# A decoder layer on one core: branch for crowded experts at the fifth pair, embedding blocks spaced, eleven tiles loaded at routing, products of ones between two-row products

## The chip, the cores and the metric

The kernel runs on one core of one Trainium2 chip, in one launch. The core has five engines with a queue each: TensorE (PE; its weight loads are shown as PEld), VectorE (DVE), ScalarE (ACT), GpSimd (POOL) and SyncE (SP), which here issues all DMAs. The metric is the time of one execution on the device in microseconds (us), as the median of several runs.

## The reference, cut to what matters

All of it is fp32, for 256 tokens of width 2048 and one layer.

```python
h = x @ w_in[i]                               # 2048 -> 9216, split into u, v, q, k, vb, ga, gb
# branch A: gated causal mixing over 128 positions; branch B: stick-breaking attention
mix = (sigmoid(ga) * ya + sigmoid(gb) * yb) @ w_o[i]
x = _layer_norm(ALPHA * x + mix, ln1_g[i], ln1_b[i])
expert_idx, gate_w = _route(xf, router_w, router_bias)    # 2 of 16 experts for each token
ffn = _moe(...)                               # (silu(x @ w_gate[e]) * (x @ w_up[e])) @ w_down[e]
ple = sigmoid(x @ ple_w_gate[i]) * (p[i] @ ple_w_proj[i]) # embedding of the layer
x = _layer_norm(ALPHA * x + ffn + ple, ln2_g[i], ln2_b[i])
```

An expert's three matrices are 2048 x 1024, 2048 x 1024 and 1024 x 2048. All sixteen experts are read, 403 MB of weights; an expert may get any number of tokens.

## The kernel before, in words

**Stages.** Up to about 600 us the kernel works on the token mixing: each weight piece is split by ScalarE and VectorE into a high and a low part, and TensorE multiplies with both. Then come the first norm and the routing (lines 510 to 663), and from about 626 us the experts. They are taken as eight pairs, numbered g = 0 to 7 (`for g in range(NP)`, line 980). Each expert has 64 places (CAP); the two experts of a pair use the two halves of TensorE's columns at the same time. A pair has four phases: `inner` "A" and "B" (line 806), eight weight tiles each, make the hidden units; `outer` "0" and "1" (line 817), four tiles each, make the output columns 0 to 1023 and 1024 to 2047. `hidden` and `turn_hidden` (lines 828, 838) stand between them. `evac` (line 847) copies an outer half out of PSUM as a high part `yh` (ScalarE) and a low part `yl` (VectorE) for each of two column blocks, and four `scatter`s (line 861) add it to `acc`: a product with the selection matrix on TensorE and an add on VectorE. The scatters of outer half "0" run as events in steps 1 to 4 of outer half "1"; those of "1" are kept in `back` and run in the next pair's phase A.

**Embedding blocks.** `ple(i)` (line 760) computes 256 of the 2048 columns of the embedding term from one weight tile and a quarter megabyte of `ple_w_proj` (in `wpt`). The list `PLE` (line 31) says after which phase of which pair each of the eight blocks runs; at (6, "B") the last one stands before outer half "0" of pair 6.

**Tiles and loads.** The pool `big` has 12 buffers of 128 x 4096 fp32 (2 MB). Weight tiles come through it in a fixed order (`loads`), one 2 MB DMA each. `done` (line 152) gives a tile's buffer back and `prefetch` (line 142) issues the next loads while `live + reserve` is below 12; `keep` reserves a buffer for something else, and `BR` takes it. A load waits on SyncE until the last reader of its buffer has finished. At routing the buffers hold `x1` (the normed rows) and `xg` (the gathered tokens of two pairs), so ten weight tiles are loaded ahead. Later `acc`, the two parts of `x1`, and `x1T` take buffers, and seven are left for weights. The pool `tp` (line 41) has five buffers of 128 x 512 fp32 for `s`, `r`, `yh`, `yl` and other short-lived tiles (`S`, line 55).

**Order of the work.** The schedule is written by hand: every engine runs its instructions in the order of the program, and the framework puts the semaphore waits in. Small jobs (gathering the next pair's tokens, the residual) stand in a list `bg`, of which `step` (line 800) takes one after each half tile.

**The branch.** `overflow` (line 927) reads the largest number of tokens of an expert into a register of each engine. If it is above 64, a loop works off the rest of all pairs with weights that it loads anew. With these inputs the branch is not taken. It stands before pair 7, in line 1007, and two buffers (`ow`, `og`) are reserved for it.

**The end.** The second norm's gain and bias, two rows of 2048 numbers, are loaded into a large tile `rows` during pair 6 and spread over the partitions by GpSimd into `gb2` (lines 1010 to 1032). After the last scatter, `busy(16)` runs sixteen products of ones that nothing reads. Then the mean and the bias come in as products with two rows (line 1072), and the eight output blocks are stored.

Of the kernel before, what the change touches and what calls it, by code (L numbers as in the profile page):

```python
# [27 lines left out]
NP = NE // 2  # L28
NB = 12

PLE = [(2, "A"), (2, "1"), (3, "A"), (4, "A"), (4, "1"), (5, "A"), (6, "A"), (6, "B")]


@with_exitstack
def trunk(ctx, tc, I, out):
# [28 lines left out]
    def C(name, shape, dt=F32):  # L64
        return consts.tile(shape, dt, name=name)
# [56 lines left out]
        keep(-1)  # L122
        return B(name, dt)

    wpt = C("wpt", [128, 2, 2, 256])

    def load_one():
        key, parts = loads[state["next"]]
        t = B("w")
        for sl, src in parts:  # L130
            if state["next"] == len(loads) - 1:
                for h in (slice(0, 2048), slice(2048, 4096)):
                    SP.dma_start(t[:, h], src[:, h])
            else:
                SP.dma_start(t[:, sl], src)  # L135
        if key[0] == "ple":
            SP.dma_start(wpt[:, key[1] % 2], I["ple_w_proj"][key[1]])
        tiles[key] = t
        state["next"] += 1
        state["out"] = state.get("out", 0) + 1  # L140
# [57 lines left out]
    POOL.iota(jp, pattern=[[1, 128]], base=0, channel_multiplier=-1, allow_small_or_imprecise_dtypes=True)  # L198
    ident = C("ident", [128, 128])
    DVE.tensor_scalar(ident, jp, 0.0, None, op0=OP.is_equal)  # L200
    tail = C("tail", [128, 128])
    DVE.tensor_scalar(tail, jp, 0.0, None, op0=OP.is_le)
    capm = C("capm", [128, 128])
    DVE.tensor_scalar(capm, jp, 0.0, None, op0=OP.is_gt)
    before = C("before", [128, 128], BF)
    DVE.tensor_copy(before, capm)
    DVE.tensor_scalar(capm, capm, 4.0e30, -1.0e30, op0=OP.mult, op1=OP.add)
    ones = C("ones", [128, 128])
    DVE.memset(ones, 1.0)
    ones_b = C("ones_b", [128, 128], BF)  # L210
    DVE.memset(ones_b, 1.0)
# [304 lines left out]
        if i == 2:  # L516
            DVE.tensor_tensor(rwg, rw, gc[:, 0, :, None].to_broadcast([128, DC, 32]), op=OP.mult)
    free(3)
    xgs = B("xg").rearrange("p (h c s) -> p h c s", h=2, c=DC)
    prefetch()  # L520

    for a in range(2):
# [140 lines left out]
        DVE.tensor_copy(cmi, cmax)  # L663


    long = {}
    Pm = C("Pm", [128, 2, 2, 128], F32R)
    PO = C("PO", [128, 2, T], F32R)
    wc = C("wc", [128, NP + 1])
    hTs = [C(f"hT{k}", [128, 4, 128]) for k in range(2)]  # L670
    pT = C("pT", [128, 2, T])
    SP.dma_start(pT, I["pT"])

    def onehot(P, at):
        for a in range(2):
# [84 lines left out]
    def ple(i):  # L760
        x1T = long["x1T"]
        w = take(("ple", i)).rearrange("p (c f) -> p c f", c=DC)
        cs = slice(i * 256, (i + 1) * 256)
        pw = AUX()
        for a in range(2):
            for c in range(2):
                PE.matmul(pw[:, a * 256:(a + 1) * 256], pT[:, c, a * 128:(a + 1) * 128], wpt[:, i % 2, c, :],
                          start=(c == 0), stop=(c == 1))
        ps = MM()
        for c in range(DC):  # L770
            for a in range(2):
                PE.matmul(ps[:, a * 256:(a + 1) * 256], x1T[:, c, a * 128:(a + 1) * 128], w[:, c, :],  # L772
                          start=(c == 0 and a == 0), stop=(c == DC - 1), skip_group_check=True)
            if c % 8 == 7:
                pop_bg()
        s = S("s")
        ACT.activation(s, ps, AF.Sigmoid)
        DVE.tensor_mul(s, s, pw)
        POOL.tensor_add(long["acc"][:, :, cs], long["acc"][:, :, cs], s.rearrange("p (a f) -> p a f", a=2))
        if i == len(PLE) - 1:  # L780
            free()
            keep()
        done()


# [102 lines left out]
    frs = C("frs", [128, 2, 2])  # L888
    cw = C("cw", [128, 2, 2])
    DVE.memset(cw, 1.0)  # L890
    rowc = C("rowc", [2, T])

    def last_columns(g, at):
        pend = None
# [32 lines left out]
    def overflow():  # L927
        most = nc.values_load(cmi[0:1, 0:1], min_val=0, max_val=T)
        with tc.If(most > CAP):
            with tc.For_i(0, NP, 1) as g:  # L930
                ce = C("ce", [128, 2, 2, 2])
                one = bass.ds(g, 1)
                for k, src in enumerate((pos, wA)):
                    DVE.tensor_copy(ce[:, k, :, None, :], src.rearrange("p a (g e) -> p a g e", e=2)[:, :, one, :])
                ow = B("ow").rearrange("p (k f) -> p k f", k=2)
                xg = B("og")[:, 0:2048].rearrange("p (c s) -> p c s", c=DC)
                with tc.For_i(1, T // CAP, 1):
                    DVE.tensor_scalar(ce[:, 0], ce[:, 0], -float(CAP), None, op0=OP.add)
                    P = Pm[:, 0]
                    onehot(P, ce[:, 0])  # L940
                    selection(P, ce[:, 1], 0, NP)
                    for f in gathers(P, xg):
                        f()
                    n = 0

                    def row(i, c):
                        nonlocal n
                        n += 1
                        SP.dma_start(ow[:, n % 2, :], xw[one, i + c // 2].rearrange("o p f -> p (o f)")[
                            :, (c % 2) * 2048:(c % 2 + 1) * 2048])  # L950
                        return ow[:, n % 2, :]

                    for k in range(2):
                        ps = [MM(), MM()]
                        for c in range(DC):
                            mm_gu(ps, xg[:, c, :], row(8 * k, c).rearrange("p (e k f) -> p e k f", e=2, k=2), c)
                        turn_hidden(hidden(ps, NP), hTs[k])
                    for k in range(2):
                        ps = [MM(), MM()]
                        for fc in range(8):  # L960
                            mm_d(ps, row(16 + 4 * k, fc).rearrange("p (e f) -> p e f", e=2), fc)
                        for f in scatters(evac(ps), 0, 1024 * k):
                            f()
                free(2)

    onehot(Pm[:, 0], pair_of(pos, 0))
    gather(Pm[:, 0], xgs[:, 0], 0)
    gather(Pm[:, 0], xgs[:, 0], 1)
    weights()
    bg.extend([lambda cp=cp: gather(Pm[:, 0], xgs[:, 0], cp) for cp in range(2, 8)])  # L970
    bg.append(lambda: selection(Pm[:, 0], pair_of(wA, 0), 0, 0))
    gb2 = rows = None
    back = []

    def ples(g, ph):
# [2 lines left out]
                ple(i)  # L978

    for g in range(NP):  # L980
        xg, i = xgs[:, g % 2], g % 2
        following = []
        if g < NP - 1:
            P = Pm[:, 1 - i]
            following.append(lambda P=P, g=g: onehot(P, pair_of(pos, g + 1)))
            if g == 0:
                following.extend([lambda P=P, x=xgs[:, 1], cp=cp: gather(P, x, cp) for cp in range(8)])
            else:
                following.extend(gathers(P, xgs[:, 1 - i]))
            following.append(lambda P=P, g=g, i=i: selection(P, pair_of(wA, g + 1), 1 - i, g + 1))  # L990
        if g == 1:
            bg.extend([None, lambda: keep(2), None, None, None, None])
# [4 lines left out]
            bg.extend([keep, None, None] + [lambda pr=pr: keep_T(pr) for pr in range(8)] + [free])  # L997
        if g == 2:
            bg.extend([lambda q=q, a=a: residual(q, a) for q in range(4) for a in range(2)])
        if g == NP - 2:  # L1000
            keep()
        if g == NP - 1:
            for f in back:
                f()
            back = []
            keep(-2)
            overflow()
        ps = inner("A", g, xg, events(back, 1))
        if g == NP - 2:
            rows = BR("rows")  # L1010
            SP.dma_start(rows[0:1, 0:D], I["ln2_g"])
            SP.dma_start(rows[0:1, D:2 * D], I["ln2_b"])
            keep()
        s = hidden(ps, g)
        ples(g, "A")
        ps = inner("B", g, xg, {3: lambda: turn_hidden(s, hTs[0])})
        s = hidden(ps, g)
        ples(g, "B")
        if g == 0:
            bg.extend(following)  # L1020
        ps = outer("0", g, {2: lambda: turn_hidden(s, hTs[1]), **({3: keep} if g == 0 else {})})
        if g == 0:
            long["acc"] = BR("acc").rearrange("p (a d) -> p a d", a=2)
        if g == NP - 2:
            gb2 = BR("gb2")
            POOL.partition_broadcast(gb2[:, 0:2048], rows[0:1, 0:D], channels=128)
            POOL.partition_broadcast(gb2[:, 2048:2560], rows[0:1, 2 * D - 512:2 * D], channels=128)
            gbr = gb2[0:2, 2560:4096]
            for k, r in enumerate((I["ln2_g"], I["ln2_b"])):
                SP.dma_start(gb2[k:k + 1, 2560:4096], r[:, 0:1536])  # L1030
            free()
            keep()
        y = evac(ps)
        ples(g, "0")
        at = events(scatters(y, i, 0, g == 0, 0 if g == NP - 1 else None), 1)
# [27 lines left out]
    ps = AUX()  # L1063
    for a in range(2):
        PE.matmul(ps[0:2, a * 128:(a + 1) * 128], cw[:, a, :], ident, start=True, stop=True)  # L1065
    ACT.activation(rowc, ps[0:2, 0:T], AF.Copy)  # L1066
    for a in range(2):
        DVE.scalar_tensor_tensor(part(3, a), part(3, a), rstd[:, a:a + 1], gb2[:, 2048:2560], op0=OP.mult, op1=OP.add)
        store(3, a)
    for n, (q, a) in enumerate((q, a) for q in range(3) for a in range(2)):  # L1070
        ps = (AUX, MM)[n % 2]()
        PE.matmul(ps, rowc[:, a * 128:(a + 1) * 128], gbr[:, q * 512:(q + 1) * 512], start=True, stop=True)  # L1072
        DVE.scalar_tensor_tensor(part(q, a), part(q, a), rstd[:, a:a + 1], ps, op0=OP.mult, op1=OP.add)  # L1073
        store(q, a)

# [63 lines left out]
```

## Time and profile before

| | |
|---|---|
| time, median of 3 runs | 1611.82 us (1609.93 to 1611.93) |
| the profiled execution's own time | 1613.37 us |
| its span in the trace | 1611.7 us |
| TensorE busy | 1571.3 us (97%) |
| VectorE, ScalarE, GpSimd busy | 546.9, 405.7, 37.8 us |
| read from HBM, written | 536.80 MB, 2.10 MB |

The trace is of one execution. "Busy" is the time in which an engine had an instruction running; a busy TensorE is not one at its peak. The granted clock (PEclk) is TensorE's, as a share of 2.4 GHz. In a row, `out<-in` names the tiles written and read, xN the number of instructions, and `<-` behind an idle time what ended it. SPq is SyncE's queue.

### The profile page before, as it was taken

What the parts mean: (1) busy time and instruction counts of PE and PEld (TensorE: products, weight loads), DVE (VectorE), ACT (ScalarE), POOL (GpSimd) and SP (SyncE); (2) the same over time, 40 slices, a digit from 0 to 9 for tenths busy, and PEclk for the clock granted to TensorE, in tenths of its full rate; (3) what the DMA queues carried; (4) which work ended last, traced back from release to release, by engine and by line L of the source; (5) the groups of instructions that cost most, each with busy time, mean ns of one, the idle gap of its engine ahead of it and who ended that gap; (6) DMA issues with size and microseconds to landing.
All of it is one profiled execution on the core that took longest, in us unless ns stands there. A gap on an engine that the chain in (4) does not pass through costs nothing. (4 is left out here: it accounts for less than half of the span.)

```text
span 1611.7 us, 17489 instructions
## 1 busy us (share of the span) xinstructions
PE 1571.3 (97%) x7226; PEld 910.5 (56%) x7226; DVE 546.9 (34%) x945; ACT 405.7 (25%) x714; POOL 37.8 (2%) x42
## 2 busy tenths in 40 slices
PE   8999999999999999999999999999999999998878
PEld 6888878888888885333334444533525533552323
DVE  5555575556565564022222112012011112101005
ACT  5455555455554442011111001001000101000000
POOL 0000000000000000000000000000000000000002
PEclk9999999999999999999999999999999999999998
DMA  9843453445546847999999999999999999999994
GB/s 383 346 157 111 182 205 147 178 160 207 186 180 263 336 188 274 416 428 427 427 428 425 414 426 429 382 428 428 427 428 427 418 429 427 427 427 389 416 429 197
DMA packets 43613, 540.08 MB, mean 335 GB/s; under 512 B 7172, under 2 KB 7172, under 8 KB 10758
## 3 DMA queue, kind: packets, MB, share of 16 engines
q1 hardware_dynamic: 43528, 538.91, 81.3%
q8 instruction: 58, 0.95, 0.3%
q14 instruction: 27, 0.22, 0.0%
HBM read 536.80 MB, written 2.10 MB: 334 GB/s over the span
## 5 line engine op out<-in xcount | busy, mean ns | idle before, releaser
L790 PE MATMUL mm<-w,xg 128*64 128x512 f32 x2048 | 467.7, 601 | 16.0 <-DMA w<-in_exp_w_dram 9.5
L283 PE MATMUL mm<-pc,xh 128*128 128x512 f32 x1152 | 362.9, 395 | 6.2 <-ACT pc L264 5.6
L265 DVE TENSOR_TENSOR pc<-w,pc 128x512 fp32r<-128x512 f32 x416 | 290.8, 709 | 199.6 <-ACT pc L264 196.9
L264 ACT ACTIVATE pc<-w 128x512 fp32r<-128x512 f32 x416 | 259.6, 630 | 234.0 <-DVE pc L265 179.7
L790 PEld LDWEIGHTS mm<-w,xg 128*64 128x64 f32 x2048 | 138.4, 137 | 277.1 <-issue 252.4
L797 PE MATMUL mm<-w,hT 128*64 128x512 f32 (+2 forms) x1088 | 236.2, 573 | 9.3 <-DMA w<-in_exp_d_last_dram 5.6
L283 PEld LDWEIGHTS mm<-pc,xh 128*128 128x128 f32 x1152 | 213.8, 189 | 51.8 <-ACT pc L264 6.0
L283 PE MATMUL mm<-pc,xl 128*128 128x512 f32 x576 | 225.4, 391 | 0.0
L797 PEld LDWEIGHTS mm<-w,hT 128*64 128x64 f32 x1088 | 72.5, 136 | 137.9 <-issue 127.4
L283 PEld LDWEIGHTS mm<-pc,xl 128*128 128x128 f32 x576 | 108.5, 188 | 22.9
L772 PE MATMUL mm<-w,x1T 128*128 128x256 f32 x512 | 112.0, 379 | 0.0
L772 PEld LDWEIGHTS mm<-w,x1T 128*128 128x128 f32 x512 | 97.2, 190 | 13.2
L834 DVE TENSOR_TENSOR s<-s,mm 128x256 f32<-128x256 f32 x32 | 13.3, 417 | 214.1 <-ACT s L833 214.1
L283 PE MATMUL mm<-pc,mixh 128*128 128x512 f32 x256 | 79.1, 390 | 0.0
L833 ACT ACTIVATE s<-mm 128x256 f32<-128x256 f32 x32 | 12.3, 384 | 235.1 <-PE mm L790 225.7
L873 DVE TENSOR_TENSOR acc<-acc,aux 128x512 f32<-128x512 f32 (+2 forms) x60 | 38.8, 650 | 94.4 <-PE aux L868 92.5
L855 ACT ACTIVATE yh<-mm 128x512 fp32r<-128x512 f32 (+1 forms) x32 | 18.5, 590 | 161.9 <-PE mm L797 161.9
L283 PEld LDWEIGHTS mm<-pc,mixh 128*128 128x128 f32 x256 | 47.9, 188 | 9.9
L283 PE MATMUL mm<-pc,mixl 128*128 128x512 f32 x128 | 49.8, 389 | 0.0
L856 DVE TENSOR_TENSOR yl<-mm,yh 128x512 fp32r<-128x512 f32 (+1 forms) x32 | 21.5, 682 | 82.1 <-ACT yh L855 81.9
L283 PE MATMUL mm<-pc,yax 128*128 128x512 f32 x192 | 44.2, 389 | 0.0
L283 PE MATMUL mm<-pc,obx 128*128 128x512 f32 x192 | 44.2, 389 | 0.0
(208 smaller groups left out, 835.0 us busy)
## 6 DMA issues: line engine op xcount, KB each, us to landing
w<-in_exp_w_dram SPq DMA_DIRECT2D x184, 2048.0 KB, 19.0
w<-in_w_in_dram SPq DMA_DIRECT2D x34, 2048.0 KB, 8.5
w<-in_w_o_dram SPq DMA_DIRECT2D x8, 2048.0 KB, 13.3
w<-in_ple_w_gate_dram SPq DMA_DIRECT2D x8, 2048.0 KB, 21.0
w<-in_exp_d_last_dram SPq DMA_DIRECT2D x7, 2048.0 KB, 39.1
w<-in_w_out_a_dram SPq DMA_DIRECT2D x4, 2048.0 KB, 8.1
w<-in_w_out_b_dram SPq DMA_DIRECT2D x4, 2048.0 KB, 7.9
w<-in_w_in_dram SPq DMA_DIRECT2D x3, 1024.0 KB, 10.9
```

The lines of the kernel that those rows point to most:

```text
L264: ACT.activation(hi, w, AF.Copy)
L265: DVE.tensor_sub(lo, w, hi.bitcast(F32))
L283: PE.matmul(ps[a], l[:, c, as_], r, start=(first and n == 0), stop=(last and n == 2))
L772: PE.matmul(ps[:, a * 256:(a + 1) * 256], x1T[:, c, a * 128:(a + 1) * 128], w[:, c, :], start=(c == 0 and a == 0), stop=(c == DC - 1), ski ...
L790: PE.matmul(ps[k][es, :], x[:, es], w[:, e, k, :], start=(c == 0), stop=(c == DC - 1), skip_group_check=True, tile_position=(0, 64 * e))
L797: PE.matmul(p[es, 0:n], hTs[fc // 4][:, fc % 4, es], w[:, e, b * n:(b + 1) * n], start=(fc == 0), stop=(fc == 7), skip_group_check=True, t ...
L833: ACT.activation(s[:, ks], pg[:, ks], AF.Sigmoid)
L834: DVE.tensor_mul(s[:, ks], s[:, ks], pg[:, ks])
L855: ACT.activation(h, p[:, 0:n], AF.Copy)
L856: DVE.tensor_sub(l, p[:, 0:n], h.bitcast(F32))
L873: DVE.tensor_add(xb, xb, ps[:, 0:n])
```

## The change

- The branch moves from before pair 7 to before pair 4 (`OVER = 4`). It gathers into the other half of `xg` and so reserves one large buffer instead of two. The two parts of `x1` give their buffers back in phase A of pair 6.
- The embedding blocks 2 and 5 move from after phase A to after phase B of their pairs (3 and 5), and block 7 from after phase B to after outer half "1" of pair 6.
- `xg` is divided: the half of pair 0 is a constant tile, the other one lies in a large tile `late` that is taken after phase B of pair 0, with `wpt`, `pT` and `rowc`. Three constant matrices lie in `hT0` until it is needed. So eleven weight tiles are loaded at routing, and pT is loaded later.
- `rows` is gone: the last 512 numbers of gain and bias are loaded into two tiles `ends` of the pool `tp`, after outer half "0" of pair 6 and before its `evac`; the first 1536 of the gain are spread from `gb2` itself.
- Between the six two-row products of the end stand five products of ones (`busy(1)`), and all six write to the `mm` buffers of PSUM.

```diff
-PLE = [(2, "A"), (2, "1"), (3, "A"), (4, "A"), (4, "1"), (5, "A"), (6, "A"), (6, "B")]
+PLE = [(2, "A"), (2, "1"), (3, "B"), (4, "A"), (4, "1"), (5, "B"), (6, "A"), (6, "1")]
+OVER = 4
...
-    xgs = B("xg").rearrange("p (h c s) -> p h c s", h=2, c=DC)
+    xgs = [C("xg0", [128, DC, 128]), None]
...
-    pT = C("pT", [128, 2, T])
-    SP.dma_start(pT, I["pT"])
+    def take_late():
+        t = BR("late")
+        xgs[1] = t[:, 0:2048].rearrange("p (c s) -> p c s", c=DC)
+        long["wp"] = t[:, 2048:3072].rearrange("p (k c f) -> p k c f", k=2, c=2)
+        long["pT"] = t[:, 3072:3584].rearrange("p (c t) -> p c t", c=2)
+        long["rowc"] = t[0:2, 3584:3840]
+        SP.dma_start(long["pT"], I["pT"])
...
         if i == len(PLE) - 1:
             free()
-            keep()
...
-                xg = B("og")[:, 0:2048].rearrange("p (c s) -> p c s", c=DC)
+                xg, f = xgs[1 - OVER % 2], 1 - OVER % 2
...
-                free(2)
+                free()
...
+        if g == OVER - 1:
+            bg.extend([None] * 20 + [keep])
         if g == NP - 2:
-            keep()
-        if g == NP - 1:
+            bg.append(lambda: (free(2), keep()))
+        if g == OVER:
             for f in back:
                 f()
             back = []
-            keep(-2)
+            keep(-1)
             overflow()
         ps = inner("A", g, xg, events(back, 1))
-        if g == NP - 2:
-            rows = BR("rows")
-            SP.dma_start(rows[0:1, 0:D], I["ln2_g"])
-            SP.dma_start(rows[0:1, D:2 * D], I["ln2_b"])
-            keep()
         s = hidden(ps, g)
         ples(g, "A")
-        ps = inner("B", g, xg, {3: lambda: turn_hidden(s, hTs[0])})
+        ps = inner("B", g, xg, {3: lambda: turn_hidden(s, hTs[0]), **({11: keep} if g == 0 else {})})
         s = hidden(ps, g)
         ples(g, "B")
         if g == 0:
+            take_late()
             bg.extend(following)
...
         if g == NP - 2:
             gb2 = BR("gb2")
-            POOL.partition_broadcast(gb2[:, 0:2048], rows[0:1, 0:D], channels=128)
-            POOL.partition_broadcast(gb2[:, 2048:2560], rows[0:1, 2 * D - 512:2 * D], channels=128)
             gbr = gb2[0:2, 2560:4096]
             for k, r in enumerate((I["ln2_g"], I["ln2_b"])):
                 SP.dma_start(gb2[k:k + 1, 2560:4096], r[:, 0:1536])
-            free()
-            keep()
+                ends = S("ends")
+                SP.dma_start(ends[0:1, :], r[:, 1536:2048])
+                POOL.partition_broadcast(gb2[:, 1536 + 512 * k:2048 + 512 * k], ends[0:1, :], channels=128)
+            POOL.partition_broadcast(gb2[:, 0:1536], gb2[0:1, 2560:4096], channels=128)
         y = evac(ps)
...
-        ps = (AUX, MM)[n % 2]()
+        ps = MM()
         PE.matmul(ps, rowc[:, a * 128:(a + 1) * 128], gbr[:, q * 512:(q + 1) * 512], start=True, stop=True)
+        if n < 5:
+            busy(1)
         DVE.scalar_tensor_tensor(part(q, a), part(q, a), rstd[:, a:a + 1], ps, op0=OP.mult, op1=OP.add)
```

## Rows read from the trace of the kernel before

**Rows 1.** The page's second part, 40 slices of the span: GB/s moved by DMA
```profile
GB/s 383 346 157 111 182 205 147 178 160 207 186 180 263 336 188 274 416 428 427 427 428 425 414 426 429 382 428 428 427 428 427 418 429 427 427 427 389 416 429 197
```

**Rows 2.** Stages: stretch, length, busy us per engine, granted clock, DMA share, GB/s
```profile
631.00:1090.00 459.00, 459.00 (x2126) 189.67 (x2126) 86.86 (x172) 50.96 (x107) 3.81 (x3) 1.00 0.99 418
...
1180.00:1220.00 40.00, 34.28 (x149) 15.80 (x146) 5.52 (x8) 2.39 (x4) 0.00 (x0) 1.00 1.00 425
...
1512.00:1573.00 61.00, 45.96 (x206) 14.39 (x204) 5.65 (x12) 3.48 (x8) 0.00 (x0) 1.00 1.01 428
```

**Rows 3.** Chain that ended last: start us, us, what
```profile
1533.47 39.10 DMA w<-in_exp_d_last_dram
...
1572.70 1.94 PE mm L797 x8
...
1591.88 1.05 PE mm L797 x16
...
1605.54 1.72 PE mm L1072 x2
```

**Rows 4.** Stretches of ten microseconds, columns as in rows 2
```profile
620.00:630.00 10.00, 9.35 (x56) 5.14 (x56) 5.49 (x31) 1.60 (x4) 0.00 (x0) 1.00 0.09 37
...
900.00:910.00 10.00, 10.00 (x50) 3.62 (x50) 2.50 (x4) 0.37 (x1) 0.00 (x0) 1.00 0.96 383
...
1020.00:1030.00 10.00, 10.00 (x48) 8.18 (x48) 0.00 (x0) 0.60 (x1) 0.00 (x0) 1.00 0.69 293
...
1030.00:1040.00 10.00, 10.00 (x50) 3.45 (x48) 1.11 (x2) 0.37 (x1) 1.27 (x1) 1.00 0.98 385
...
1480.00:1490.00 10.00, 7.60 (x24) 2.65 (x26) 0.00 (x0) 0.00 (x0) 0.00 (x0) 0.66 0.73 304
...
1490.00:1500.00 10.00, 10.00 (x48) 3.61 (x46) 0.00 (x0) 0.00 (x0) 0.00 (x0) 1.00 0.90 342
```

**Rows 5.** SyncE's waits, 870 to 900, 1000 to 1045: total us, times, longest
```profile
SPq L135 <- PE mm L772: 16.2, 1, 16.2
...
SPq L135 <- PE mm L772: 15.3, 1, 15.3
```

**Rows 6.** TensorE's timeline, three stretches: start us, us, operation, count
```profile
1425.99 1.99 PE L767 MATMUL aux<-wpt,pT 128*128 128x256 f32 x8
...
1427.82 13.98 PE L772 MATMUL mm<-w,x1T 128*128 128x256 f32 x64
...
1487.55 24.70 PE L790 MATMUL mm<-w,xg 128*64 128x512 f32 x114
...
1559.89 0.66 PE L842 MATMUL aux<-ident,s 128*128 128x128 f32 x4
```

**Rows 7.** Line 929, the branch: instruction, count, ns min/median/max, first and last start
```profile
L929 SPq EVENT_SEMAPHORE  x8: 17/17/17, 1476.3 to 1490.0; - x8
...
L929 PEldq COMPARE_BRANCH  x1: 6658/6658/6658, 1475.4 to 1475.4; - x1
```

**Rows 8.** TensorE's timeline, end of pair 6 and begin of pair 7
```profile
1464.84 0.50 PE L868 MATMUL aux<-yh,PO 128*128 128x512 f32 x1
...
1475.48 0.40 PE L868 MATMUL aux<-yl,PO 128*128 128x512 f32 x1
...
1482.40 1.12 PE L790 MATMUL mm<-w,xg 128*64 128x512 f32 x2 [6.53 <-PEq L929]
```

**Rows 9.** Tile wpt, loaded behind weight tiles: from issue to landing
```profile
DMA to landing us min/median/max: 15.7/25.4/30.0
```

**Rows 10.** GpSimd's timeline, the broadcast of 512 columns
```profile
1455.39 0.80 POOL L1027 PARTITION_BROADCAST gb<-rows  x1
```

**Rows 11.** TensorE's timeline, products of ones and two-row products of the end
```profile
1593.83 3.62 PE L530 MATMUL aux<-ones_b 128*128 128x512 bf16 x16
...
1598.44 1.12 PE L1072 MATMUL aux<-gb,rowc 2*128 2x512 f32 x2 [0.46 <-ACT rowc L1066]
...
1600.26 1.86 PE L1072 MATMUL aux<-gb,rowc 2*128 2x512 f32 x2
```

More of the change, by code (lines that the diff above doesn't have):

```diff
@@ L123, in BR @@
         return B(name, dt)
-    wpt = C("wpt", [128, 2, 2, 256])
+    long = {}
     def load_one():
@@ L136, in load_one @@
         if key[0] == "ple":
-            SP.dma_start(wpt[:, key[1] % 2], I["ple_w_proj"][key[1]])
+            SP.dma_start(long["wp"][:, key[1] % 2], I["ple_w_proj"][key[1]])
         tiles[key] = t
@@ L200, in trunk @@
     DVE.tensor_scalar(ident, jp, 0.0, None, op0=OP.is_equal)
-    tail = C("tail", [128, 128])
+    hT0 = C("hT0", [128, 4, 128])
+    tail = hT0[:, 0, :]
     DVE.tensor_scalar(tail, jp, 0.0, None, op0=OP.is_le)
-    capm = C("capm", [128, 128])
+    capm = hT0[:, 1, :]
     DVE.tensor_scalar(capm, jp, 0.0, None, op0=OP.is_gt)
@@ L207, in trunk @@
     DVE.tensor_scalar(capm, capm, 4.0e30, -1.0e30, op0=OP.mult, op1=OP.add)
-    ones = C("ones", [128, 128])
+    ones = hT0[:, 2, :]
     DVE.memset(ones, 1.0)
@@ L663, in weights @@
         DVE.tensor_copy(cmi, cmax)
-    long = {}
     Pm = C("Pm", [128, 2, 2, 128], F32R)
@@ L669, in trunk @@
     wc = C("wc", [128, NP + 1])
-    hTs = [C(f"hT{k}", [128, 4, 128]) for k in range(2)]
-    pT = C("pT", [128, 2, T])
-    SP.dma_start(pT, I["pT"])
+    hTs = [hT0, C("hT1", [128, 4, 128])]
+    def take_late():
[5 more added lines that the diff above has]
+        SP.dma_start(long["pT"], I["pT"])
     def onehot(P, at):
@@ L766, in ple @@
             for c in range(2):
-                PE.matmul(pw[:, a * 256:(a + 1) * 256], pT[:, c, a * 128:(a + 1) * 128], wpt[:, i % 2, c, :],
+                PE.matmul(pw[:, a * 256:(a + 1) * 256], long["pT"][:, c, a * 128:(a + 1) * 128], long["wp"][:, i % 2, c, :],
                           start=(c == 0), stop=(c == 1))
@@ L890, in trunk @@
     DVE.memset(cw, 1.0)
-    rowc = C("rowc", [2, T])
     def last_columns(g, at):
@@ L935, in overflow @@
                 ow = B("ow").rearrange("p (k f) -> p k f", k=2)
-                xg = B("og")[:, 0:2048].rearrange("p (c s) -> p c s", c=DC)
+                xg, f = xgs[1 - OVER % 2], 1 - OVER % 2
                 with tc.For_i(1, T // CAP, 1):
                     DVE.tensor_scalar(ce[:, 0], ce[:, 0], -float(CAP), None, op0=OP.add)
-                    P = Pm[:, 0]
+                    P = Pm[:, f]
                     onehot(P, ce[:, 0])
-                    selection(P, ce[:, 1], 0, NP)
-                    for f in gathers(P, xg):
-                        f()
+                    selection(P, ce[:, 1], f, NP)
+                    for fn in gathers(P, xg):
+                        fn()
                     n = 0
@@ L961, in overflow @@
                             mm_d(ps, row(16 + 4 * k, fc).rearrange("p (e f) -> p e f", e=2), fc)
-                        for f in scatters(evac(ps), 0, 1024 * k):
-                            f()
-                free(2)
+                        for fn in scatters(evac(ps), f, 1024 * k):
+                            fn()
+                free()
     onehot(Pm[:, 0], pair_of(pos, 0))
-    gather(Pm[:, 0], xgs[:, 0], 0)
-    gather(Pm[:, 0], xgs[:, 0], 1)
+    gather(Pm[:, 0], xgs[0], 0)
+    gather(Pm[:, 0], xgs[0], 1)
     weights()
-    bg.extend([lambda cp=cp: gather(Pm[:, 0], xgs[:, 0], cp) for cp in range(2, 8)])
+    bg.extend([lambda cp=cp: gather(Pm[:, 0], xgs[0], cp) for cp in range(2, 8)])
     bg.append(lambda: selection(Pm[:, 0], pair_of(wA, 0), 0, 0))
-    gb2 = rows = None
+    gb2 = None
     back = []
@@ L980, in trunk @@
     for g in range(NP):
-        xg, i = xgs[:, g % 2], g % 2
+        xg, i = xgs[g % 2], g % 2
         following = []
@@ L986, in trunk @@
             if g == 0:
-                following.extend([lambda P=P, x=xgs[:, 1], cp=cp: gather(P, x, cp) for cp in range(8)])
+                following.extend([lambda P=P, cp=cp: gather(P, xgs[1], cp) for cp in range(8)])
             else:
-                following.extend(gathers(P, xgs[:, 1 - i]))
+                following.extend(gathers(P, xgs[1 - i]))
             following.append(lambda P=P, g=g, i=i: selection(P, pair_of(wA, g + 1), 1 - i, g + 1))
@@ L1065, in trunk @@
         PE.matmul(ps[0:2, a * 128:(a + 1) * 128], cw[:, a, :], ident, start=True, stop=True)
+    rowc = long["rowc"]
     ACT.activation(rowc, ps[0:2, 0:T], AF.Copy)
```

## The prediction

> **What bounds the kernel now.** I read the page's slices first, then busy time and DMA rate by stage, the chain of waits, the waits of SyncE's queue, and last the stretches of ten microseconds in which the rate falls. From slice 17 on the DMA engines move about 428 GB/s in nearly every slice [rows 1], one 2 MB weight tile in 4.90 us (2.097 MB by 428). TensorE looks busy too: never idle from 631 to 1090 us, at 1180 to 1220 waiting 5.7 of 40 us, and from 1512 to 1573 waiting 15 of 61 us at full rate [rows 2]. The chain that ends last goes through a tile that was on its way for 39.1 us, which is eight tiles in flight at 4.9 [rows 3]. So the end is set by when the last tiles land. TensorE's time counts only where it runs so far behind that all seven tile buffers are full and the queue runs dry. That costs rate: at 620 to 630 us (all ten tiles loaded, 9.1 us lost), at 900 to 910 (1.0 lost), at 1020 to 1040 (10 x (1 - 293/428) = 3.2, and 1.0 more: 4.2 lost) and at 1480 to 1500 (2.9 + 2.0 = 4.9 lost) [rows 4].
>
> **Eleven tiles at routing.** One tile more falls into the dry stretch at 620 us, 4.9 us ahead. But the next dry stretch, at 900, ends when TensorE ends the first embedding block: SyncE waits 16.2 us for it [rows 5]. TensorE does not wait before that, so this end stays; a queue that is 4.9 us ahead only runs dry 4.9 us earlier. The gain is between 0 and 4.9, and I take 0.7, since not much over the 1.0 lost there can come back. The later load of pT (256 KB, 0.6 us) goes the same way.
>
> **Blocks spaced.** The stop at 1020 to 1040 is the third block, 15.3 us of SyncE waiting for it [rows 5], one phase of eight tiles after the second block. Its new place is eight tiles later: TensorE takes a tile in 3.47 us (24.70 x 16 / 114) [rows 6] and DMA brings one in 4.90, so the buffers hold 8 x 1.43 = 11.4 us less when the block comes, more than the 10 by which it fills them (15.8 [rows 6] less 5.5 for its own 2.25 MB). I take the whole 4.2 back. The same move for the sixth block is worth at most its stop, under 1 us; cost nothing, because the lead there is in the buffers.
>
> **The branch.** It costs two things. TensorE's compare-and-branch lasts 6.66 us [rows 7], and its matmuls stand still from 1475.9 to 1482.4 [rows 8]; then the granted clock is 0.66 over ten microseconds [rows 4], and about 5.2 us run at 1.2 instead of 2.4 GHz, 2.6 lost. Together 9.1. SyncE goes through eight semaphores from 1476.3 to 1490.0 [rows 7], one for each DMA lane that the skipped body uses: it loads nothing until all that it issued has landed. That is the 4.9 us of rate. Queued behind it on SyncE are the loads of the next tiles. At pair 4, the fifth, both prices are the same, since the wait is for landing and not for free buffers. The DMA loss only changes its place. TensorE then reaches the fourth block 9.1 later against 4.9 for DMA, so 4.2 us more lie in full buffers, besides the 4.2 no longer lost at the third block: a new stop at the fourth block of 0 to 4.2 (no stop before; the third block's is the nearest row). I take 2.0. The Trainium skill, "Advanced Engine Details and Errata", section "Control Flow Timing", gives about 108 ns for a compare-and-branch. The row says 6.66 us on TensorE, so here the measurement decides; by the page's figure TensorE would not fall behind, the new stop would not be there and the sum would be 2.0 less.
>
> **The gain rows through `ends`.** This step decides. Before, `rows` is a large tile. Now two small tiles `ends` come from the pool of five [128, 512] buffers, after pair 6's first outer half, and directly behind them `evac` takes four more: yh, yl, yh, yl. Six tiles, five buffers, and the first yh, yl, yh are read only by later scatters: the last yl must go where an `ends` was, and VectorE may not write it before GpSimd has broadcast that `ends`. The broadcast waits for a 2 KB transfer that stands behind every tile in flight. A transfer of this kind, `wpt`, lands 15.7 to 30.0 us after issue, median 25.4 [rows 9]. Here eight tiles are out (seven buffers, two more freed in this pair, one of them for gb2): up to eight times 4.9, 39. Behind yl on VectorE stand the adds of the first two scatters; on TensorE the third scatter, which starts at 1464.84 now [rows 8], about 8.5 us after the half ended, and everything after it. So TensorE stops for 7 (15.7 - 8.5) to 30 us (39 - 8.5). Since TensorE is nearly waiting for DMA there, I take the long end: it goes on when the eighth tile, the third of pair 7, has landed, plus 1 us (0.80 for the broadcast [rows 10], some tenths for yl).
>
> **The sum.** Before, SyncE's last semaphore at 1490.0 [rows 7] is the landing of pair 7's fifth tile; the third landed two tiles earlier, about 1479.5 as the last one before a stop comes late. From there to the last matmul at 1592.9 [rows 3] are 113.4: 21 tiles x 4.9 = 102.9, the branch 4.9, and 5.6 left over for the last tile's matmuls. Changed, this tile lands at 1479.5 + 4.9 (branch now ahead of it) - 4.2 - 0.7 + 2.0 = 1481.5, and TensorE goes on at 1482.5. Its own work from the third scatter on: rest of the half with the four back scatters 11.0 (1464.84 to 1475.88 [rows 8]); the last block 15.8 [rows 6], which now stands here; sixteen inner tiles 55.5 and a turn 0.7; four outer tiles and a turn 14.5 [rows 6]; the last columns 20.2 (1572.70 to 1592.93 [rows 3]). Sum 117.7, end 1600.2. DMA can't undercut this: the buffers are full through the last block, so it stops again, and the tiles behind that block land as late. Against 1592.9 that is 7.3 later.
>
> **Products of ones.** The first two two-row products take 1.8 us together, the others 1.72 each; after the second the clock falls to 1.2 GHz although TensorE is never idle [rows 3, 11]. Five products of ones of 0.22 (3.62 / 16) [rows 11] are put between. If they hold the clock: 1.8 + 4 x 0.86 + 5 x 0.22 = 6.3 against 8.7, 2.4 saved. If it falls at the same place: 1.8 + 0.22 + 4 x 1.72 + 4 x 0.43 = 10.6, 1.9 lost. Before it fell TensorE ran sixteen products of ones and then only narrow ones [rows 11]; at three quarters busy with wide ones it kept 1.00 for 61 us [rows 2]. The changed stretch is between the two. I take 0.5 saved: it falls, but later. VectorE's 0.75 per product is hidden either way.
>
> Net +6.8 on the profiled execution's 1613.37 us (span 1611.70), so 1620.2; the median of the runs shown is 1.55 lower, which gives **1618.6**.
>
> **Rivals.** (B) The wait for `ends` is not there or short: the one-row transfer gets through ahead of the tiles. For it: it fills one ring only, and nothing here shows a one-row transfer's landing. Against: `wpt` [rows 9]. The Trainium skill, "DMA: Bandwidth & Descriptors", section "Queues, rings and completion order", has ring order on each DMA engine but no order of completion over the sixteen; by that a one-row transfer may pass the slowest ring's tile share, and no run here shows by how much. It decides from the point at which the broadcast ends within 8.5 us. Then DMA sets the end: 1481.5 + 102.9 + 5.6 = 1590.0, 2.9 earlier, with the ones 3.4: 1608.4. (C) B, and also the eleventh tile counts whole and no new stop comes: 1479.5 + 4.9 - 4.2 - 4.9 = 1475.3, end 1583.8, 9.1 earlier, 2.4 from the ones: 1600.3. Against it: the stop at 900 us [rows 4, 5]. (D) The wait is there and everything beside it goes badly: new stop 4.2, ones lose 1.9: 7.3 + 2.2 + 1.9 = 11.4 later, 1623.2.
>
> **Chances.** Forecast 0.60, B 0.27, C 0.05, D 0.08. A measurement of this kernel can't tell less than 0.2%, 3.2 us, from no change. The forecast is slower in 0.50 of its 0.60 (an early landing brings the rest under 3.2); B is faster in 0.17, the same in 0.10; C faster; D slower: faster 0.22, same 0.20, slower 0.58. The range takes in the forecast, D's price and most of B: 1607 to 1623; the likeliest case alone, 1614 to 1623.
>
> **What would show it.** In the changed trace: VectorE's last yl of pair 6's first half waiting for GpSimd's broadcast, and TensorE idle over 15 us before that half's third scatter; GpSimd waiting for a DMA there; the eight semaphores and the 6.7 us branch at about 1090; no stop at the third block; a dry stretch at the first block larger than now; a dry stretch at the last block. The forecast is wrong if TensorE goes through that half in under 20 us. It is then B, and the last tile's landing says how much the rest was worth.

## The result, and the profile after

Median 1623.82 us (4 runs, 1619.94 to 1624.94) against 1610.95 for the kernel before: ratio 1.0076, 95% interval 1.0057 to 1.0095. The same program run again (e1) gave 1.0065 (1.0051 to 1.0079). So the change makes the kernel 0.65 to 0.76% slower, 10.5 to 12 us. The profiled execution took 1619.94 us (span 1618.2), 6.6 more than the profiled one of before, but most executions take three to five more than that; the experiments say why.

The page's slices, GB/s, answer to [rows 1]. Dips stand at 890 to 930, at 1090 to 1130 and at 1490 to 1540 us (slices 23, 28 and 38).
```profile
GB/s 386 341 156 117 187 204 154 159 171 194 207 170 259 355 175 327 422 427 427 427 427 427 369 427 428 426 427 376 428 427 428 425 428 427 428 428 418 336 427 176
```
The same by stretches of ten microseconds, columns as in [rows 2, 4]:
```profile
620.00:630.00 10.00, 9.34 (x58) 5.03 (x55) 5.43 (x30) 1.37 (x3) 0.00 (x0) 1.00 0.48 201
890.00:900.00 10.00, 10.00 (x50) 5.94 (x51) 2.29 (x4) 0.60 (x1) 1.27 (x1) 1.00 0.66 244
900.00:910.00 10.00, 10.00 (x52) 3.58 (x49) 2.19 (x4) 0.37 (x1) 0.00 (x0) 1.00 0.97 370
1020.00:1030.00 10.00, 10.00 (x50) 3.55 (x51) 0.43 (x1) 0.37 (x1) 0.00 (x0) 1.00 1.02 433
1100.00:1110.00 10.00, 10.00 (x46) 3.68 (x42) 1.14 (x3) 1.50 (x3) 0.00 (x0) 1.00 0.66 247
1110.00:1120.00 10.00, 10.00 (x46) 3.98 (x46) 1.96 (x5) 1.96 (x4) 0.00 (x0) 1.00 0.96 401
1140.00:1150.00 10.00, 10.00 (x48) 8.81 (x47) 0.00 (x0) 0.00 (x0) 0.00 (x0) 1.00 1.01 429
1460.00:1470.00 10.00, 0.00 (x0) 0.00 (x0) 0.00 (x0) 0.00 (x0) 0.00 (x0) 0.50 1.01 426
1480.00:1490.00 10.00, 10.00 (x41) 3.80 (x38) 2.43 (x4) 1.19 (x2) 0.18 (x1) 0.90 0.98 403
1490.00:1500.00 10.00, 10.00 (x49) 8.79 (x47) 0.00 (x0) 0.00 (x0) 0.00 (x0) 1.00 0.69 297
1500.00:1510.00 10.00, 10.00 (x46) 5.26 (x44) 1.38 (x2) 0.60 (x1) 1.27 (x1) 1.00 0.48 169
```
Against [rows 4]: the eleventh tile fills part of the gap at 620; the stop at the first block has grown to 10 x (1 - 244/428) + 10 x (1 - 370/428) = 4.3 + 1.4 us; the third block's stop at 1020 is gone; the branch now costs 4.2 + 0.6 us of rate at 1100 to 1120; the fourth block (1140) stops nothing. Then TensorE stands still at 1460 while DMA runs at 426, and at 1480 to 1510 the queue runs dry behind full buffers.

SyncE's waits, answering to [rows 5]: total us, times, longest, for 870 to 920 and then 1000 to 1045.
```profile
SPq L137 <- PE mm L781: 16.1, 1, 16.1
...
SPq L137 <- PE mm L798: 37.9, 11, 5.0
```
The wait for the first block is as long as before, and the 15.3 us for the third one is gone.

The branch at its new place, answering to [rows 7]: instruction, count, ns min/median/max, first and last start.
```profile
L936 SPq EVENT_SEMAPHORE  x8: 17/17/17, 1096.7 to 1108.1; - x8
...
L936 SPq COMPARE_BRANCH  x1: 50/50/50, 1086.8 to 1086.8; - x1
...
L936 PEldq COMPARE_BRANCH  x1: 5952/5952/5952, 1090.7 to 1090.7; - x1
```
TensorE's compare-and-branch takes 5.95 us (5.93 in e2 is the shortest; 5.8 to 6.3 us without a matmul in the other profiles with the branch there), the other engines' 45 to 72 ns. The Trainium skill, "Advanced Engine Details and Errata", section "Control Flow Timing", gives about 108 ns. The four other engines' 45 to 72 ns lie below that and TensorE's 5.95 us far above it, so here the measurement decides.

The wait for `ends`. SyncE's timeline first, then what GpSimd, VectorE and TensorE wait for (start us, us, operation, [idle before <- what ended it]):
```profile
1449.46 0.31 SPq L1033 DMA_DIRECT2D gb<-in_ln_g_dram  x1
1454.37 0.22 SPq L1035 DMA_DIRECT2D ends<-in_ln_g_dram  x1
1459.21 0.22 SPq L1033 DMA_DIRECT2D gb<-in_ln_b_dram  x1
1464.16 0.22 SPq L1035 DMA_DIRECT2D ends<-in_ln_b_dram  x1
...
1477.04 1.48 POOL L1036 PARTITION_BROADCAST gb<-ends  x2 [75.87 <-DMA ends<-in_ln_b_dram]
...
1477.87 0.69 DVE L864 TENSOR_TENSOR yl<-mm,yh 128x512 fp32r<-128x512 f32 x1 [33.91 <-POOL gb L1036]
...
1453.85 0.50 PE L876 MATMUL aux<-yh,PO 128*128 128x512 f32 x1
1478.62 0.79 PE L876 MATMUL aux<-yl,PO 128*128 128x512 f32 x1 [24.28 <-DVE yl L864]
1479.34 3.22 PE L805 MATMUL mm<-w,hT 128*64 128x512 f32 x8
...
1596.69 1.09 PE L805 MATMUL mm<-w,hT 128*64 128x128 f32 x16
```
This is the forecast's step as it was told: the last `yl` waits for GpSimd, GpSimd for the rows' transfers, and TensorE stands for 24.3 us before it can finish the third scatter [rows 8 has it at 1464.84 without a stop]. The four small loads are not issued in a row: each waits on SyncE 4.4 to 4.7 us for another DMA to land, so the last of them leaves 14.7 us after the first. By the transfers' records in the trace that delay made little difference: all four land together, at 1476.3 to 1476.9, just behind the first of the sixteen shares (1475.9) of the 2 MB tile issued before them at 1444.6, whose last share lands at 1479.4. The first row of `ends` was on its way for 22.1 us, the second for 12.7. After the stop the eight matmuls of a half tile take 3.22 us instead of 1.94: the granted clock is half until 1481.97. The last matmul with weights ends at 1597.8, 4.9 later than in [rows 3], and from there to the end of the span are 20.4 us instead of 18.8.

### The profile page after: what moved, and what is told of

The parts are those of the page before. It is cut to its first block, busy times and chain, and to the rows that moved or that the text cites. A ratio compares the mean times of both kernels' runs of the same rounds, so it can differ in the third digit from the quotient of the medians.

```text
span 1618.2 us, 17503 instructions
## 1 busy us (share of the span) xinstructions
PE 1570.7 (97%) x7231; PEld 910.3 (56%) x7231; DVE 547.2 (34%) x945; ACT 405.7 (25%) x714; POOL 37.9 (2%) x43
## 5 line engine op out<-in xcount | busy, mean ns | idle before, releaser
L798 PE MATMUL mm<-w,xg 128*64 128x512 f32 x1024 | 233.8, 601 | 5.9 <-PEq L936 5.9
L798 PE MATMUL mm<-w,late 128*64 128x512 f32 x1024 | 231.0, 597 | 0.0
L798 PEld LDWEIGHTS mm<-w,xg 128*64 128x64 f32 x1024 | 69.0, 137 | 134.0 <-issue 126.2
L798 PEld LDWEIGHTS mm<-w,late 128*64 128x64 f32 x1024 | 69.0, 136 | 131.0 <-issue 130.4
## 6 DMA issues: line engine op xcount, KB each, us to landing
w<-in_w_in_dram SPq DMA_DIRECT2D x3, 1024.0 KB, 10.4
```

What stands on the lines that cost most here:

```text
L798: PE.matmul(ps[k][es, :], x[:, es], w[:, e, k, :], start=(c == 0), stop=(c == DC - 1), skip_group_check=True, tile_position=(0, 64 * e))
```

## The experiments

All were run beside the kernel before, and each ratio is to it. "Last matmul" is the end of the last one with weights; the "tail" is what lies between it and the end of the span.

**e1, the changed kernel again.** No edit.

> The changed kernel as it is, for a second profile. Its profiled execution took 1619.94 us with a mean granted clock of 0.988, the three others 1623.2 to 1624.9 with 0.985. 0.003 of 1621 us at half clock instead of full is 9.7 us more at 1.2 GHz, 4.9 us lost. Theory 1: it is lost behind the 24 us stop of TensorE at the ends wait: the clock stays half after the stop for some 10 us longer than to 1481.97, and the last matmul ends at about 1602 instead of 1597.8. Theory 2: it is lost behind the last matmul, among the two-row products: last matmul at 1597.8 as before, and 23 to 25 us from it to the end of the span instead of 20.4. Theory 3: the branch, whose half-rate stretch was 3.4 us there. Median expected 1623.5 to 1624.5 under all three.

1622.92 us (1620.09 to 1623.58), ratio 1.0065 (1.0051 to 1.0079). The profiled execution was again an early one (1620.09; last matmul 1598.1, tail 20.3), so it could not tell the theories apart. e11 and e12 do.

**e2, `ends` elsewhere.** The half of `xg` that pair 6 no longer needs takes the two rows.
```diff
-                ends = S("ends")
+                ends = xgs[0].rearrange("p c s -> p (c s)")[:, 512 * k:512 * k + 512]
```


> The two ends rows go into the idle half of xg instead of two of the five tp buffers; nothing else. My theory: the whole stop of TensorE in pair 6 (24 us) and all of its loss comes from yl waiting for the broadcast. Without it DMA sets the end: third tile of pair 7 at 1479.5, + 102.9 + 5.6 = last matmul 1588.0, 4.9 earlier than before, and the tail with ones 1.6 longer: 1610.95 - 3.3 = 1607.7, clock 0.993 or more. Rival: DMA sets the end anyway and the stop only hides in it: within 2 us of the changed kernel, 1622 or more. Rival: the slower clock is one of the tail: then 4 us of the loss stay, about 1611.5.

1612.2 us, ratio 1.0000 (0.9991 to 1.0009): 10.7 less than e1. The rows come no earlier, but nobody waits for them (GpSimd, then TensorE at the third scatter and at the end):
```profile
1477.23 1.48 POOL L1036 PARTITION_BROADCAST gb<-xg  x2 [76.05 <-DMA xg<-in_ln_b_dram]
...
1453.91 0.50 PE L876 MATMUL aux<-yh,PO 128*128 128x512 f32 x1
1454.25 0.40 PE L876 MATMUL aux<-yl,PO 128*128 128x512 f32 x1
...
1586.84 1.09 PE L805 MATMUL mm<-w,hT 128*64 128x128 f32 x16
```
The last matmul ends at 1587.9, against 1588.0 expected. The total is 4.5 over what was expected. Of that, 1.7 is that the kernel before itself took 1612.64 beside these runs instead of 1610.95. The rest lies behind that matmul (a tail of 22.0 us here, 20.4 expected): the products of ones cost more than the 1.6 that I had read from the one trace; e4 says how much.

**e3 and e4, no products of ones,** in the changed kernel and on top of e2.
```diff
-        if n < 5:
-            busy(1)
```


> The changed kernel without the five products of ones. From the trace (tail 20.4 against 18.8 us): 1.6 less, 1622.2. Rival, that the ones hold the clock and save up to 2.4: 1626. Rival, that the slower clock of most executions comes from the stretch of the ones: about 1618, and clock 0.988 in all.

> Both undone, ends in the idle half of xg and no products of ones: 1607.7 - 1.6 = 1606.1 if the two add up; with the rival that the ones hold the clock, about 1610.

e3: 1618.82 us, ratio 1.0044 (1.0030 to 1.0057), 4.1 less than e1. e4: 1607.46 us, ratio 0.9970 (0.9961 to 0.9980), 4.7 less than e2. So the products cost 4.1 to 4.7 us; the expectation of 1.6 was a miss, and the rival that they save something is out. e3's third reading had about the right time, 1618, but not the clock of 0.988 in all: four of its five executions have 0.986 to 0.987. The two costs add up: 11.4 from e3 to e4, 10.7 from e1 to e2. e4 takes 0.30% less than the kernel before (0.20 to 0.39%).

**e6, the products of ones made small.** In e2, 8 columns instead of 512.
```diff
-            busy(1)
+            PE.matmul(AUX()[:, 0:8], ones_b, ones_b[:, 0:8], start=True, stop=True)
```


> As the kernel with the ends rows in xg (1612.2), but each of the five products of ones has 8 columns instead of 512. Theory 1, that a product of ones costs what its 512 columns take (0.22 us each at full rate, 0.43 at half): nearly nothing is left, 1607.5 to 1608.5. Theory 2, that it costs the overlap of two fp32 products with one another (1.12 us alone against 0.86 in a row): at least 0.26 each at full and more at half rate stay, 1610 to 1611.5.

1610.65 us, ratio 0.9988 (0.9979 to 0.9997): 3.2 of the 4.7 stay against e4, 2.9 against e8, which is e4 again and ran beside it. So it is not the products' own columns alone. TensorE's timeline at the end of the kernel before, then of e4, e6 and e12 (the changed kernel):
```profile
1599.40 1.02 PE L1072 MATMUL mm<-gb,rowc 2*128 2x512 f32 x2
```
```profile
1593.67 6.45 PE L1078 MATMUL mm<-gb,late 2*128 2x512 f32 x12 [0.46 <-ACT late L1072]
```
```profile
1593.23 1.12 PE L1078 MATMUL mm<-gb,late 2*128 2x512 f32 x2 [0.46 <-ACT late L1072]
1594.28 0.18 PE L1080 MATMUL aux<-ones_b 128*128 128x8 bf16 x1
1594.39 1.77 PE L1078 MATMUL mm<-gb,late 2*128 2x512 f32 x2
...
1600.34 0.19 PE L1080 MATMUL aux<-ones_b 128*128 128x8 bf16 x1
...
1602.46 0.19 PE L1080 MATMUL aux<-ones_b 128*128 128x8 bf16 x1
```
```profile
1605.01 1.12 PE L1078 MATMUL mm<-gb,late 2*128 2x512 f32 x2 [0.46 <-ACT late L1072]
1606.06 0.39 PE L533 MATMUL aux<-ones_b 128*128 128x512 bf16 x1
1606.38 1.12 PE L1078 MATMUL mm<-gb,late 2*128 2x512 f32 x2
...
1610.14 2.07 PE L1078 MATMUL mm<-gb,late 2*128 2x512 f32 x2
...
1612.68 2.07 PE L1078 MATMUL mm<-gb,late 2*128 2x512 f32 x2
```
In a row a two-row product comes every 0.86 us at full (1600.26 [rows 11] less 1599.40) and every 1.72 at half clock [rows 3]. With a product of ones behind each it comes every 1.37 (1606.38 less 1605.01) and every 2.54 (1612.68 less 1610.14): 0.51 and 0.82 more, though a one in a row is 0.22. A two-row product that stands alone lasts 1.12 and 2.07; between two of its kind part of that is covered. With 8 columns the step is still 2.12 at half clock (1602.46 less 1600.34), and 1.16 at full (1594.39 less 1593.23). Slower steps also leave fewer products before the clock falls. In the fourteen profiles it falls 7.0 to 10.6 us after the last matmul, 9.0 in the mean, and the products begin 5.5 after it: 3.5 us hold 4.1 of them in a row (3.5/0.86), 3.0 with 8 columns, 2.6 with 512, and each that falls to half clock costs 0.86 more. For 512 columns that makes an estimate of 2.6 x 0.51 + 2.4 x 0.82 + 1.5 x 0.86 = 4.6, for 8 columns 3.0 x 0.30 + 2 x 0.40 + 1.1 x 0.86 = 2.6, against 4.7 and 3.2 measured; it hangs on that mean.

The trace's clock records give the price without a mean. In the seven profiles without these ones (the kernel before, e3, e4, e5, e7 to e9) the tail and the time from the last matmul to the fall add up to 26.1 to 26.2 us, however early the clock falls; in the six with ones of 512 columns to 30.7 to 31.0; in e6 to 28.4. So at the same fall five ones of 512 columns cost 4.5 to 4.8 us and five of 8 columns 2.2, about half. The rest of e6's 2.9 to 3.2 may be an earlier fall: 7.0 us after the last matmul in its profile, 9.8 in e4's. The kernel before and e5 write the two-row products to `aux` and `mm` in turn and have the same sum as the others, so the move to `mm` alone costs nothing.

What is covered in a row is not shown: e6 keeps the weight load of each one too. In the kernel before the load of a two-row product's weights starts 0.42 us before the product, behind a one it starts with it (1604.69 in the first profile of the changed kernel). No run tells a lost overlap of products from a lost overlap of weight loads.

**e5, the two blocks alone.** The kernel before with two places of the list changed.
```diff
-PLE = [(2, "A"), (2, "1"), (3, "A"), (4, "A"), (4, "1"), (5, "A"), (6, "A"), (6, "B")]
+PLE = [(2, "A"), (2, "1"), (3, "B"), (4, "A"), (4, "1"), (5, "B"), (6, "A"), (6, "B")]
```


> The kernel before with nothing but the third and the sixth embedding block moved from after phase A to after phase B of their pairs. My theory: the stop at 1020 to 1040 goes, worth the 4.2 us of rate that was lost there, and none comes at the new place: last matmul 4.2 earlier, about 1607.6 (ratio 0.9974). Rival: the lost rate turns up again at a later block, since TensorE has the same work: 1611 to 1612, and a slice below 400 GB/s at 1060 to 1090 or 1300 to 1330.

1608.17 us, ratio 0.9974 (0.9965 to 0.9983), which is 4.2 us of 1612 (2.7 to 5.6). The third block, in which the kernel before loses its 4.2, now runs at 1040 to 1060. At its old and at its new place the rate is whole or nearly so:
```profile
1020.00:1030.00 10.00, 10.00 (x50) 3.63 (x50) 0.42 (x1) 0.37 (x1) 0.00 (x0) 1.00 1.00 426
...
1040.00:1050.00 10.00, 10.00 (x48) 7.87 (x45) 1.72 (x4) 0.77 (x2) 0.00 (x0) 1.00 1.02 431
1050.00:1060.00 10.00, 10.00 (x48) 7.08 (x48) 0.69 (x1) 0.60 (x1) 1.27 (x1) 1.00 0.99 423
```
The stretches that the rival named, 1060 to 1090 and 1300 to 1330, are at 427 as well, and the last matmul of this profile ends at 1589.4, 3.5 earlier than in the kernel before.

**e7, the branch before pair 6,** in e4.
```diff
-OVER = 4
+OVER = 6
```


> As the kernel with the ends rows in xg and without products of ones (1607.5), but the branch stands before pair 6 instead of pair 4. My theory: the branch loses 4.9 us of loading wherever it stands and TensorE's delay is covered by the buffers: 1607.5, within 1.5 us. Rival, the new stop of my prediction at the block one phase behind the branch, which did not come at pair 4 and could come here: up to 4.2 more, 1611.7, with a slice below 350 GB/s at 1390 to 1410. Rival, that a branch close to the end is dearer, because the end has no block left in which TensorE's delay is made up: 1610.

1608.8 us, ratio 0.9981 (0.9972 to 0.9989), 1.3 more than e4 (1.1 more than e8, which ran beside it), last matmul 1.7 later (1589.9). Stretches at the branch and one phase behind it:
```profile
1350.00:1360.00 10.00, 9.76 (x30) 3.42 (x31) 0.49 (x2) 0.58 (x1) 0.00 (x0) 0.71 0.86 362
1360.00:1370.00 10.00, 10.00 (x48) 3.77 (x46) 1.92 (x4) 2.28 (x5) 0.00 (x0) 1.00 0.60 223
...
1390.00:1400.00 10.00, 10.00 (x48) 8.81 (x47) 1.12 (x3) 0.14 (x1) 0.00 (x0) 1.00 1.00 426
```
The branch loses 1.5 + 4.8 = 6.3 us of loading here, against 4.8 at pair 4 in the changed kernel; the block behind it, at 1390 to 1410, loses nothing here either (426 and 431). That is within the 1.5 us that I allowed, and the place matters little. Why it loses 1.5 more is not shown.

**e8 and e9, ten tiles instead of eleven,** in e4. e8 counts one buffer as kept at routing; e9 takes the large tile there.
```diff
     xgs = [C("xg0", [128, DC, 128]), None]
+    late = B("late")                  # e9; in e8: keep()
+    DVE.memset(late[0:1, 0:1], 0.0)
     prefetch()
```


> As the kernel with the ends rows in xg and without products of ones (1607.5), but one buffer is kept back at routing, so that ten tiles are loaded ahead as before. My theory: the eleventh is worth 0 to 0.7, since the loading stops at the first block at 890 to 910 anyway: 1607.5 to 1608.2, and nearly no stop at 890 to 910. Rival: it counts whole, 4.9: 1612.4.

> e8 kept its buffer back only in the count of the loads; the trace shows eleven tiles issued by 609 us all the same, so it was a second run of e4. Here the large tile late is taken at routing, so the buffer is gone and ten are loaded. My theory: the eleventh tile is worth 0 to 0.7, 1607.5 to 1608.3, and the stop at 890 to 910 shrinks from 5.7 to about 1 us. Rival: it counts whole, 4.9: 1612.4.

e8: 1607.75 us, ratio 0.9973 (0.9964 to 0.9982), but with eleven loads issued by 609 us: the count held a load back in the program, not in the queue, because the kept buffer was itself the next to be handed out. It tells nothing of the tile. e9: 1607.73 us, ratio 0.9975 (0.9966 to 0.9984), 0.3 more than e4. Its stretches:
```profile
620.00:630.00 10.00, 9.35 (x58) 5.04 (x55) 5.44 (x30) 1.37 (x3) 0.00 (x0) 1.00 0.03 12
890.00:900.00 10.00, 10.00 (x50) 5.94 (x51) 2.29 (x4) 0.60 (x1) 1.27 (x1) 1.00 1.01 429
900.00:910.00 10.00, 10.00 (x52) 3.58 (x49) 2.18 (x4) 0.37 (x1) 0.00 (x0) 1.00 0.98 397
```
With ten tiles 620 to 630 is dry and the first block stops 0.7 us; with eleven it is the other way round. The tile is worth 0.3 by the medians and 0.8 by the ratios, neither clear of nothing with runs that spread over 3 us; the rival's 4.9 is out.

**e10, the stop filled.** The changed kernel, with products of ones through most of the wait.
```diff
+        if g == NP - 2:
+            third = at[3]
+            at[3] = lambda: (busy(100), third())
```


> The changed kernel with 100 products of ones (0.22 us each, some 22.6 us) put ahead of the third scatter of pair 6, so that TensorE works through most of the stop at the ends wait and comes out of it with a warm clock. Theory 1, that the executions above 1620 lose their time to a longer stretch at half clock behind the stop: the clock stays at 1.00 through the stop, the median falls to 1619 or less, the mean clock rises above 0.992 in every execution. Theory 2, that they lose it behind the last matmul: median stays within 1 us of 1623 and the mean clock stays more than 0.003 below that of the first, profiled execution. Theory 3, that the loss is in waiting for the rows themselves (they land later in those executions): median stays at 1621 or more with a mean clock of 0.992 or more.

1620.93 us (1618.16 to 1622.95), ratio 1.0058 (1.0045 to 1.0072), 2.0 less than e1 (1.1 by the ratios, 2.5 to 2.8 less than e11 and e12 beside it), with a mean granted clock of 0.992 to 0.995 instead of 0.985 to 0.988. TensorE:
```profile
1453.49 21.76 PE L533 MATMUL aux<-ones_b 128*128 128x512 bf16 x100
...
1478.21 0.49 PE L876 MATMUL aux<-yl,PO 128*128 128x512 f32 x1 [2.73 <-DVE yl L864]
1478.63 1.94 PE L805 MATMUL mm<-w,hT 128*64 128x512 f32 x8
...
1594.73 1.09 PE L805 MATMUL mm<-w,hT 128*64 128x128 f32 x16
```
`yl` comes as late as without them, but the next half tile takes 1.94 us instead of 3.22 and the last matmul ends at 1595.8. So the low clock behind the stop costs about 2 us of the 10.7 and the wait itself the rest. None of the three theories is met whole: the clock rose as theory 1 asked, but the median came to theory 3's 1621 instead of 1619. The low clock there explains about half of what lay between the first profile and the median; theory 1 had put all of it there.

**e11 and e12, two more looks at the changed kernel.**

> The changed kernel once more, for a profile of an execution of 1622 us or more: it shows where the half-clock stretch is longer than in the profile of 1619.94 (23.9 us about the stop, 10 to 12 at the end). Theory 1: behind the stop, to 1485 or later. Theory 2: at the end, beginning 7 to 9 us behind the last matmul instead of 10.5.

> The same look once more, with the same expectations: theory 1, the half clock behind the stop lasts to 1485 or later in an execution of 1622 us or more; theory 2, the half clock at the end begins earlier behind the last matmul.

1623.71 and 1623.42 us: these are the usual executions. e12 behind the stop and at its last matmul:
```profile
1479.15 0.80 PE L876 MATMUL aux<-yl,PO 128*128 128x512 f32 x1 [24.21 <-DVE yl L864]
1479.88 3.68 PE L805 MATMUL mm<-w,hT 128*64 128x512 f32 x8
...
1598.38 1.09 PE L805 MATMUL mm<-w,hT 128*64 128x128 f32 x16
```
Both theories hold, and each explains half. The clock rises at 1485.1 instead of 1482.0 (e11: 1485.4), and the last matmul ends at 1599.5 (e11: 1599.8), 1.7 later. And it falls 8.5 us after the last matmul instead of 10.5, so one two-row product more runs at half clock: tail 22.25 instead of 20.45, another 1.8. Together 3.5 of the 3.5 us between 1619.94 and 1623.42.

## Why the prediction was wrong, step by step

The direction and the mechanism were right. The time fell 0.8 us outside the range, and the failed step is **the products of ones**: "I take 0.5 saved", between 2.4 saved and 1.9 lost. They cost 4.1 (e1, e3) to 4.7 us (e2, e4), over twice the upper bound. I priced a one by what it takes in a row (0.22, at half clock 0.43), and the two-row products by what they take in a row. The price of an operation between two of another kind stood in [rows 11]: a two-row product alone lasts 1.12 us, not 0.86. That they might hold the clock fails as well. It fell 8.5 to 10.6 us after the last matmul with ones of 512 columns and 7.0 to 10.4 without.

- **`ends`.** The stop was 24.3 us (forecast 7 to 30, at the long end). TensorE went on at 1478.6 to 1479.5 instead of 1482.5. It did not wait for the third tile of pair 7 to land whole, as I took it: that tile lands at 1479.4 instead of 1481.5, since the new stop did not come, and the rows are through 2.6 us before its last share. That much of rival B is true, a row passes the slowest share of a tile, but not the tile. The records of the kernel before could have shown it: its two rows of gain and bias, issued at 1453.0 and 1453.3, landed at 1468.2 and 1468.4, right behind the first share (1467.1) of the tile issued before them. Its own work to the last matmul took 119.2 to 120.3 us instead of 117.7, because the forecast gave it full clock from the first product on. The two errors nearly cancel: last matmul 1597.8 to 1599.8, forecast 1600.2. Taken away (e2), it is worth 10.7 us.
- **The new stop at the fourth block**, 2.0: did not come, neither in the changed kernel nor, behind the branch, in e7. The low end of its range was right.
- **Blocks spaced**, 4.2: e5 has 0.26%, 4.2 us. **Eleven tiles**, 0.7: 0.3 to 0.8, not clear of nothing. The first block's end stayed where it was and the queue ran dry earlier, as told. **The branch**, 4.9 of rate moved from one place to the other: 4.2 + 0.6.
- **Without the wait** the DMA sum gave 1588.0 for the last matmul (rival B's 1590.0 less the new stop); e2 had 1587.9. So B's path, which needs the rows early, is that of e2, and its total was wrong by the ones. C, the eleventh tile whole, fails by e9. D has almost the measured time, but by another sum: its 4.2 for the stop at the fourth block is not there.
- **From the profile to the median.** I took 1.55 off, as the profiled execution of before lay that much above its median. Of the changed kernel the first profile lay 3.9 below the median, so the two profiled times alone understate the loss. That makes up the miss: between 1618.6 and 1623.8 lie 5.2 us, and against the forecast e12 has 4.0 more of tail (22.25 instead of 18.76 less 0.5) and 0.7 less up to the last matmul; 1.55 are this offset, and the median is 0.4 above e12. The profile of the kernel before was a draw too: its clock fell 7.4 us after the last matmul, that of the changed kernel 10.5, so that the two tails, 18.8 and 20.5, hide 3.1 of the 4.8 that the ones cost. In e12 the last matmul is 6.6 and the tail 3.5 later than in [rows 3], the 10.1 us between the spans.

What remains without the two losses, e4's 0.30%, can't be told from the spacing alone (e5's 0.26%, 0.17 to 0.35%).

## What to carry to other kernels

Before a small short-lived tile is put into a rotating pool, count how many tiles are taken behind it before its reader is done: one 2 KB row behind full-size loads held up an engine for 24 us, and the same row in an idle corner cost nothing (e2). An instruction put between two of another kind can cost more than its own length in a row: look up how long these last alone. And where the clock falls near the end or behind a stop, one profile is one draw: compare medians before a few microseconds are explained.

## What was not expected of the hardware

- The low clock's end moves between executions of one program: behind the same stop it rose 3.3 to 3.7 us after TensorE went on (the first profile, e1, e3) or 5.9 us (e11, e12), and at the end it fell 7.0 to 10.6 us after the last matmul over all profiles. The rise is worth 1.7 us of the last matmul's end, the fall up to 3.3 (tails of 15.8 to 19.1 us without ones). The Trainium skill, "TensorE: Matmul & The Clock Gate", section "Part 1: The HAM clock gate (the "warmup" mystery)", says of the rise that the same kernel differs from run to run; the traces agree, and show it of the fall too.
- SyncE waited 4.4 to 4.7 us for an older load to land before it issued each of four small ones, with free destinations. By the trace's records SyncE's loads take turns over eight semaphores, and each of the four left 0.02 to 0.08 us after the older load on its own semaphore had landed (1449.40 for the first, which starts at 1449.46). That fits a limit of eight loads outstanding; no experiment tried it.
- A product of 8 columns between fp32 products of two rows costs at the same fall of the clock about half of what one of 512 costs (2.2 against 4.5 to 4.8 us for five), though its own columns are a 64th; by the medians more of it stays (2.9 to 3.2 against 4.7 us for five).
